# Two-block transformer kernel: split order of summed weight blocks on ScalarE, squares summed on VectorE, low parts ahead of adding DMAs

## Chip, cores and metric

One core of one Trainium2 chip runs the whole program in one launch. The metric is the device time of the program in microseconds (us), the median of several runs. TensorE (PE) does the matmuls, VectorE (DVE), ScalarE (ACT) and GpSimd (POOL) the elementwise work; SyncE (SP) and GpSimd issue DMAs. Each engine works through one queue of its own, in an order fixed when the program is built.

## What is computed

The reference runs two blocks of two layers each over x of 1 x 512 x 1024 in float32. For this change the feed-forward parts and the norms around them matter:

```python
# first block, each layer (sandwich norms)
h = h + rmsnorm(mixed, norm_gains[layer, 1])
hn = rmsnorm(h, norm_gains[layer, 2])
h = h + rmsnorm(swiglu_ffn(hn, ffn_w_in[layer], ffn_w_out[layer]), norm_gains[layer, 3])
# second block, each layer (norm ahead of each part)
x = x + mixer(rms_norm(x, mix_norm))
x = x + conv_ffn(rms_norm(x, ffn_norm[layer]), ffn_w_up[layer], ...)
```

The up-projection of each feed-forward part is 1024 x 5632, the down-projection 2816 x 1024. rmsnorm divides by the root of the mean square over the 1024 channels.

## The kernel before

**Layout.** Activations stand with channels on the 128 partitions: h is 128 x 8 x 512, eight chunks of channels by 512 tokens. Many steps work on half of the tokens (256) at a time; "half 0" and "half 1" below.

**Three matmuls for one.** Each fp32 operand is held as a high part (rounded to fp32r) and a low part (what the rounding left); a product is high x high + high x low + low x high. A weight block of 128 x 1024 is loaded into a buffer `raw0`, `raw1`, ... and split in `pump`: ACT casts it to the high part in a slot `W0` to `W3` (or `R0`, `X0`, ...), line 237, and DVE subtracts to get the low part, line 238.

**Seven products for eight.** The up-projection (`plan_up`, `product`, `up_first`, `up`) is done for each column pair j = 0 to 10 as seven products p = 1 to 7 over sums of quarter blocks, Strassen's way. Products 1 and 2 and product 3 of the early pairs take a quarter of the weights as loaded; 5, 6, 7 and 4 take sums. The sums are made in the raw buffer itself by adding DMAs: once the low part of a block is made, a GpSimd DMA with `accum_op=add` (line 240) adds the next quarter onto the same buffer, and the next block is split from it. So one buffer goes load, split, add, split, add, split. A block (j, p) is a `Spec`; `add` is the quarter that is to be added after its split. For pairs 0 to 3 the first sum, that of product 5, is not made behind a split but right after the load, by DMAs that `flush` issues (line 201).

**The order of the blocks.** `up_order` gives products 1 and 2 of pairs 0 to 3 first (eight products, run in `up_first`), then (0,5) (1,5) (0,3) (1,3) (0,6) (1,6) (0,7) (1,7) (0,4) (1,4), then the same for pairs 2 and 3, then the steady part. Slot W3 takes block 0 of the buffer that held `ya`, half of the norm's y, and so is free when `combine` (below) has read ya for the last time.

**Norms.** `norm_chain` is a generator whose steps are set between the matmuls of other work: each `yield t` puts the next step t us of matmul columns later on a planned PE clock (`tick`, 2.4 columns per ns). In the two sandwich layers a chain has two norms in a row: `rstd` of the mixer's (or feed-forward's) output y, `spread` of the result over all partitions, then y is scaled and added to h (lines 433 and 434), ACT squares h (line 435), DVE adds some of the squares (line 437), and `rstd` runs again on h:

```python
parts = [a[:, i] for a in (sums, tmp) for i in range(2)]
...
for j in range(2):
    for i, a in enumerate(parts):
        nc.tensor.matmul(st[:, j : j + 1], a[:, j * P : (j + 1) * P], self.invn, ...)
```

Squares of chunks 0, 2, 4 are added pairwise on DVE, those of chunks 6 and 7 are left in `tmp`; the four 128 x 256 parts are summed over partitions by PE (line 399). `rstd` ends with a DVE add of epsilon (line 403) and a GpSimd power (line 405); `spread` (line 412) puts the result on PE again. Then `combine` forms the left operands of the seven products (s1 to s4 and others) on DVE and ACT, lines 467 to 509, in an order written out by hand.

Each of the two layers has such chains twice, for two halves each: in `sandwich_out` (before the up-projection, while `up_first` runs in half 1) and in `sandwich_ffn` (after the down-projection). That makes eight chains with two norms. The second block's stages (`pre_out`) have one norm per chain and no line 435.

**What orders the queues.** PE's order is that of the program text (`in_order`). On the other engines a list scheduler orders instructions at build time: of those that are ready by its own estimate it issues the one with the smallest priority number, which is its place in the text; `high_priority(n)` moves it n places ahead. `FIRST` is 200; the norms use 400. `issue_after(ins)` puts what it wraps behind `ins` in the queue of `ins`'s engine, with no wait for it to finish.

Of the kernel before, what the change touches and what calls it, by code (L numbers as in the profile page):

```python
# [17 lines left out]
P = 128  # L18
# [20 lines left out]
class Rows:  # L39


    def __init__(self, *parts):
        self.parts = parts
# [15 lines left out]
class Spec:  # L59
# [1 line left out]

    def __init__(self, tag, nk, nc, slots, early, raw, loads=(), prep=None, add=None, ends=()):
        self.tag, self.nk, self.nc, self.slots, self.early = tag, nk, nc, slots, early
        self.raw, self.loads, self.prep, self.add, self.ends = raw, loads, prep, add, ends


class Net:
# [147 lines left out]
    def pump(self, most=99):  # L217
        nc = self.nc
        for _ in range(most):
            if self.n_split == len(self.specs):  # L220
                break
            self.load_more()
            s = self.specs[self.n_split]
            slot = next((x for x in s.slots if x in self.free), None)
            if slot is None or any(k not in self.raws for k in s.loads):
                return
            if any(key in s.loads for key, *_ in self.adds):
                self.flush(self.last_pow)
            self.free.discard(slot)
            if s.prep:  # L230
                out, x, y, eng = s.prep
                getattr(nc, eng).tensor_add(self.raws[out][1], self.raws[x][1], self.raws[y][1])
            n = s.nk * s.nc
            reg = self.slot_at[slot]
            hi, lo = reg[:, :n], reg[:, 1024 : 1024 + n]
            raw = self.raws[s.raw][1][:, :n]
            nc.scalar.copy(hi, raw)  # L237
            (nc.gpsimd if s.early else nc.vector).tensor_sub(lo, raw, hi.bitcast(F32))  # L238
            if s.add is not None:
                nc.gpsimd.dma_start(raw.rearrange("p (k c) -> p k c", k=s.nk), s.add, accum_op=ALU.add)  # L240
            for k in s.ends:
                self.raw_free.append(self.raws.pop(k)[0])
            r = dict(k=s.nk)
            self.loaded[self.n_split] = Chunk(
                slot, hi.rearrange("p (k c) -> p k c", **r), lo.rearrange("p (k c) -> p k c", **r), s.nk)
            self.n_split += 1
        self.load_more()
# [142 lines left out]
            nc.scalar.activation(sq[:, :n], src, AF.Square)  # L390
            eng.tensor_add(acc[:, cols], acc[:, cols], sq[:, :n])  # L391

    def rstd(self, parts):

        nc = self.nc
        st = self.mbank()
        for j in range(2):
            for i, a in enumerate(parts):
                nc.tensor.matmul(st[:, j : j + 1], a[:, j * P : (j + 1) * P], self.invn, start=i == 0,
                                 stop=i == len(parts) - 1)  # L400
        with self.tc.high_priority(400):
            v = self.sm.tile([P, 2], F32, tag="v", name="v")
            nc.vector.tensor_scalar_add(v, st[:, 0:2], EPS)
            r = self.sm.tile([P, 2], F32, tag="r", name="r")
            self.last_pow = nc.gpsimd.tensor_tensor(r, v, self.mhalf[:, 0:2], ALU.pow)
        return r
# [9 lines left out]
    def norm_chain(self, acc, half, gain, pool=None, y=None, acc_y=None, work=None):  # L416


        nc = self.nc
        cols = slice(half * HS, (half + 1) * HS)  # L420
        if y is not None:
            yield 2.6
            r = self.rstd([acc_y[:, cols]])
            if half and work is not None:
                self.flush(self.last_pow)
            yield 2.0
            R = self.spread(r)[:, :HS].unsqueeze(1).to_broadcast([P, 2, HS])
            with self.tc.high_priority(400):
                sums = pool.tile([P, 2, HS], F32, tag="sums", name="sums", bufs=2)
                for c in range(0, NC, 2):  # L430
                    tmp = y[:, c : c + 2, cols]
                    hv = self.h[:, c : c + 2, cols]
                    nc.vector.tensor_mul(tmp, tmp, R)
                    (nc.vector.tensor_sub if work is None else nc.vector.tensor_add)(hv, hv, tmp)
                    nc.scalar.activation(tmp if c else sums, hv, AF.Square)
                    if c in (2, 4):
                        nc.vector.tensor_add(sums, sums, tmp)
            parts = [a[:, i] for a in (sums, tmp) for i in range(2)]
            yield 7.0
        else:  # L440
            yield 5.4 if half and work is not None else 2.6
            parts = [acc[:, cols]]
        r = self.rstd(parts)
        if half and work is not None:
            self.flush(self.last_pow)
        yield 1.4 if y is not None else 2.8 if half and work is not None else 2.0
        R = self.spread(r)
        with self.tc.high_priority(400):
            if work is not None:
                with self.tc.manual_schedule(engines={mybir.EngineType.DVE}):  # L450
                    self.combine(pool, work, half, gain, R)
                return
            for c in range(NC):
                tmp = self.nrm.tile([P, HS], F32, tag="tmp", name="tmp", bufs=3)
                nc.vector.scalar_tensor_tensor(tmp, self.h[:, c, cols], gain[:, c : c + 1], R[:, :HS], ALU.mult,
                                               ALU.mult)
                self.split(tmp, self.res(c, 0, half), self.res(c, 1, half))
# [293 lines left out]
    def plan_up(self, tag, w, engines=None):  # L751


        wv = w.rearrange("(k p) c -> p k c", p=P)
        W = ["W0", "W1", "W2", "W3"]
        early = [W[:3] + RS, RS + W[:3]]
        src = lambda j, r, c: wv[:, 4 * r : 4 * r + 4, c * FF + j * 256 : c * FF + (j + 1) * 256]
        a, b, c = {}, {}, {}
        first, rest = self.up_order()

        def load(j, r, c, add=None):
            return self.raw(src(j, r, c), 4, 256, True, add)

        def spec(j, p, raw, **kw):
            slots = early[j > 0] if (j, p) in first else W[:3] if (j, p) in rest[-3:] else W
            self.specs.append(Spec(tag, 4, 256, slots, False, raw, **kw))

        for j, p in first + rest:
            e = j < self.EARLY
            if p == 1:  # L770
                k = load(j, 0, 0)
                if e:
                    spec(j, p, k, loads=[k], ends=[k])
                else:
                    a[j] = k
                    spec(j, p, k, loads=[k], add=None if engines else src(j, 0, 1))
            elif p == 2:
                k = load(j, 1, 0)
                spec(j, p, k, loads=[k], ends=[k])
            elif engines:  # L780
                if p == 5:
                    if e:
                        a[j] = load(j, 0, 0)
                    b[j] = load(j, 0, 1)
                    spec(j, p, a[j], loads=[a[j], b[j]], prep=(a[j], a[j], b[j], engines[0]))
                elif p == 3:
                    c[j] = load(j, 1, 1)
                    spec(j, p, c[j], loads=[c[j]])
                elif p == 6:
                    spec(j, p, a[j], prep=(a[j], a[j], c[j], engines[1]))  # L790
                elif p == 7:
                    spec(j, p, b[j], prep=(b[j], b[j], c[j], engines[2]), ends=[b[j], c[j]])
                else:
                    k = load(j, 1, 0)
                    spec(j, p, a[j], loads=[k], prep=(a[j], a[j], k, engines[3]), ends=[a[j], k])
            elif p == 5:
                if e:
                    a[j] = load(j, 0, 0, src(j, 0, 1))
                spec(j, p, a[j], loads=[a[j]], add=src(j, 1, 1))
            elif p == 3:  # L800
                c[j] = load(j, 1, 1)
                last = j == NF // 2 - 1
                spec(j, p, c[j], loads=[c[j]], add=None if last else src(j, 0, 1), ends=[c[j]] if last else [])
                if last:
                    c[j] = load(j, 1, 1, src(j, 0, 1))
            elif p == 6:
                spec(j, p, a[j], add=src(j, 1, 0))
            elif p == 7:
                spec(j, p, c[j], loads=[c[j]], ends=[c[j]])
            else:  # L810
                spec(j, p, a[j], ends=[a[j]])
# [1333 lines left out]
```

## Time and profile before

| what | value |
|---|---|
| median of 3 runs | 2576.38 us (2574.99 to 2578.72) |
| the profiled execution's own time | 2584.16 us |
| its span, first to last instruction | 2582.3 us |
| PE busy | 2467.4 us (96% of the span) |
| DVE / ACT / POOL busy | 1527.4 / 1168.2 / 550.1 us |
| mean granted TensorE clock | 0.98 of full speed |

Times in the trace are counted from the first instruction of the profiled execution. "Idle before" is time in which an engine stood still ahead of an instruction, with what ended it. The granted clock is a share of 2.4 GHz: 0.50 is 1.2 GHz, 1.00 is 2.4 GHz, and a value between them a stretch that had both.

### The profile page before, as it was taken

To read this page: it belongs to the slowest core of one execution; us is meant where nothing else is said; L and a number is where in the kernel's file an instruction comes from. 1 tells how busy PE (TensorE), PEld (TensorE's weight loads), DVE (VectorE), ACT (ScalarE), POOL (GpSimd) and SP (SyncE) were. 2 spreads that over 40 slices of the span, in tenths; PEclk is the share of its full clock that TensorE was granted. 3 is DMA by queue.
4 is the path that set the end of the run, shared out by engine and by line. 5 is a ranking of instruction groups with operands and counts; after the bars stand their busy time and mean duration, and the time that the engine had idled before them with its cause. 6 is when DMAs were issued, how large, how long until landed. Compare 5 with 4: busy or idle time off the path is not lost.

```text
span 2582.3 us, 40752 instructions
## 1 busy us (share of the span) xinstructions
PE 2467.4 (96%) x16477; PEld 2205.8 (85%) x16477; DVE 1527.4 (59%) x2400; ACT 1168.2 (45%) x1920; POOL 550.1 (21%) x500
## 2 busy tenths in 40 slices
PE   8999889999999998799999989899999999999999
PEld 6778889998898988799988759899888768989978
DVE  5766565563555555655625675787834445697841
ACT  4545445553232324455533553566622433466731
POOL 0000133310011111233101221455300000264400
PEclk9999989999999999899999999999999999999999
DMA  4223379944112123799531213989541223889741
GB/s 136 83 74 99 105 136 191 184 108 127 50 58 74 58 90 94 142 191 186 111 127 62 65 58 106 160 172 175 119 129 57 65 58 106 181 167 177 146 142 29
DMA packets 304886, 297.00 MB, mean 115 GB/s; under 512 B 11645, under 2 KB 294875, under 8 KB 304699
## 3 DMA queue, kind: packets, MB, share of 16 engines
q1 hardware_dynamic: 210235, 197.57, 25.0%
q0 software_dynamic: 94384, 96.81, 24.1%
q8 instruction: 129, 2.11, 0.3%
q14 instruction: 58, 0.48, 0.1%
q10 hardware_dynamic: 80, 0.03, 0.0%
HBM read 292.24 MB, written 2.13 MB: 114 GB/s over the span
## 4 chain that ended last, share of the span: by engine, by line
PE 43%; DVE 6%; DMA 3%; issue 3%; ACT 2%; POOL 1%; ACTq 0%; DVEq 0%; POOLq 0%
PE g L334 34%; PE a L334 4%; DMA raw<-in_ffn_w_up_dram 3%; DVE W L238 2%; ACT W L237 1%; PE m L334 1%; PE m L1900 1%; DVE u L932 1%; DVE s L932 1%; DVE s L933 0%; ACT s L931 0%; PE a L1883 0%; PE a L1209 0%; DVE R L173 0%; DVE u L933 0%
## 5 line engine op out<-in xcount | busy, mean ns | idle before, releaser
L238 DVE TENSOR_TENSOR W<-raw,W 128x1024 fp32r<-128x1024 f32 x455 | 573.2, 1263 | 458.9 <-ACT W L237 456.1
L237 ACT CAST W<-raw 128x1024 fp32r<-128x1024 f32 x455 | 472.4, 1040 | 603.6 <-PE g L334 272.7
L334 PE MATMUL g<-R,W 128*128 128x512 f32 (+2 forms) x3048 | 685.0, 375 | 7.8 <-DVE W L238 4.8
L334 PEld LDWEIGHTS g<-R,W 128*128 128x128 f32 (+1 forms) x3048 | 511.4, 190 | 105.1 <-issue 6.1
L334 PE MATMUL g<-s,W 128*128 128x256 f32 x3840 | 479.2, 284 | 27.6 <-ACT hid L947 13.6
L334 PEld LDWEIGHTS g<-s,W 128*128 128x128 f32 x3840 | 467.9, 191 | 32.5 <-ACT hid L947 16.5
L334 PE MATMUL g<-W,R 128*128 128x256 f32 (+1 forms) x1224 | 233.9, 337 | 0.0
L334 PEld LDWEIGHTS g<-W,R 128*128 128x128 f32 x1224 | 181.8, 191 | 25.3 <-issue 6.7
L334 PE MATMUL a<-a,W 128*128 128x256 f32 x1536 | 196.1, 283 | 3.5 <-DVE c L841 2.2
L334 PEld LDWEIGHTS a<-a,W 128*128 128x128 f32 x1536 | 188.8, 190 | 4.3 <-DVE c L841 2.4
L240 POOL DMA_DIRECT2D raw<-in_ffn_w_in_dram x78 | 100.4, 1289 | 228.5 <-DVE W L238 212.4
L240 POOL DMA_DIRECT2D raw<-in_ffn_w_up_dram x78 | 103.5, 1368 | 121.5 <-DVE W L238 114.5
L334 PE MATMUL g<-a,W 128*128 128x256 f32 x864 | 109.6, 282 | 0.3
L965 POOL TENSOR_TENSOR hid<-u,s 128x512 f32<-128x512 f32 x44 | 82.6, 1887 | 118.4 <-ACT s L962 111.8
L334 PE MATMUL g<-R,R 128*128 128x256 f32 (+1 forms) x792 | 107.0, 291 | 0.7 <-ACT ya L657 0.7
L334 PEld LDWEIGHTS g<-a,W 128*128 128x128 f32 x864 | 105.6, 189 | 1.1 <-DVE a L475 0.9
L238 DVE TENSOR_TENSOR X<-raw,X 128x1024 fp32r<-128x1024 f32 (+1 forms) x46 | 49.6, 1085 | 95.6 <-ACT X L237 95.6
L391 POOL TENSOR_TENSOR acc<-acc,sq 128x512 f32<-128x512 f32 x19 | 30.0, 1581 | 355.1 <-ACT sq L390 355.0
L334 PEld LDWEIGHTS g<-R,R 128*128 128x128 f32 x792 | 101.2, 195 | 2.7 <-ACT ya L657 1.1
L334 PE MATMUL g<-R,X 128*128 128x256 f32 (+1 forms) x576 | 94.0, 320 | 0.0
L334 PEld LDWEIGHTS g<-R,X 128*128 128x128 f32 x576 | 83.1, 190 | 7.8
L237 ACT CAST X<-raw 128x1024 fp32r<-128x1024 f32 (+1 forms) x46 | 42.9, 937 | 98.6 <-PE g L334 72.3
(413 smaller groups left out, 3451.2 us busy)
## 6 DMA issues: line engine op xcount, KB each, us to landing
raw<-in_ffn_w_in_dram POOLq DMA_DIRECT2D x88, 512.0 KB, 6.3
raw<-in_ffn_w_up_dram POOLq DMA_DIRECT2D x88, 512.0 KB, 6.3
raw<-in_ffn_w_in_dram SPq DMA_DIRECT2D x76, 512.0 KB, 4.9
raw<-in_ffn_w_up_dram SPq DMA_DIRECT2D x76, 512.0 KB, 4.8
raw<-in_ffn_w_out_dram SPq DMA_DIRECT2D x40, 512.0 KB, 3.5
raw<-in_ffn_w_down_dram SPq DMA_DIRECT2D x40, 512.0 KB, 4.0
raw<-in_hgrn_w_in_dram SPq DMA_DIRECT2D x32, 512.0 KB, 4.1
raw<-in_fox_w_in_dram SPq DMA_DIRECT2D x24, 512.0 KB, 3.8
```

The source lines that it names most:

```text
L237: nc.scalar.copy(hi, raw)
L238: (nc.gpsimd if s.early else nc.vector).tensor_sub(lo, raw, hi.bitcast(F32))
L240: nc.gpsimd.dma_start(raw.rearrange("p (k c) -> p k c", k=s.nk), s.add, accum_op=ALU.add)
L334: self.nc.tensor.matmul(*args, **kw, **(dict(skip_group_check=True) if skip else {}))
L391: eng.tensor_add(acc[:, cols], acc[:, cols], sq[:, :n])
L932: nc.vector.scalar_tensor_tensor(u[:, 1:], src[:, : S - 1], w(1), u[:, 1:], ALU.mult, ALU.add)
L965: nc.gpsimd.tensor_mul(hid[:, t], u, s)
L1900: mm(po[i * 64 : i * 64 + 64, h * HS : (h + 1) * HS], q[:, 2 * b + h, ck * 64 : (ck + 1) * 64], state[h], start=True, stop=True)
```

## The change

Three edits. First, every block of an up-projection is marked `up`, and those of products 4 to 7 `summed`; the high part of a summed block is put on ACT behind the last `up` high part that was traced before it, or behind the last square of the norm's half 1 in `sandwich_out`, whichever was traced later. Second, the low part of a block that an adding DMA follows gets priority 200. Third, `norm_chain` adds all squares on DVE (chunk 6's too, then the two columns of `sums` into one 128 x 256 accumulator), and `rstd` takes that one operand.

```diff
@@ Spec
+        self.up, self.summed = up, summed
@@ pump
-            nc.scalar.copy(hi, raw)
-            (nc.gpsimd if s.early else nc.vector).tensor_sub(lo, raw, hi.bitcast(F32))
+            with self.tc.issue_after(self.last_hi.ins) if s.summed else ExitStack():
+                hi_made = nc.scalar.copy(hi, raw)
+            if s.up:
+                self.last_hi = hi_made
+            with self.tc.high_priority(self.FIRST) if s.add is not None else ExitStack():
+                (nc.gpsimd if s.early else nc.vector).tensor_sub(lo, raw, hi.bitcast(F32))
@@ rstd
-    def rstd(self, parts):
+    def rstd(self, acc):
...
-            for i, a in enumerate(parts):
-                nc.tensor.matmul(st[:, j : j + 1], a[:, j * P : (j + 1) * P], self.invn, start=i == 0,
-                                 stop=i == len(parts) - 1)
+            nc.tensor.matmul(st[:, j : j + 1], acc[:, j * P : (j + 1) * P], self.invn, start=True, stop=True)
@@ norm_chain
-                    nc.scalar.activation(tmp if c else sums, hv, AF.Square)
-                    if c in (2, 4):
+                    square = nc.scalar.activation(tmp if c else sums, hv, AF.Square)
+                    if c:
                         nc.vector.tensor_add(sums, sums, tmp)
-            parts = [a[:, i] for a in (sums, tmp) for i in range(2)]
+                nc.vector.tensor_add(acc[:, cols], sums[:, 0], sums[:, 1])
+            if half and work is not None:
+                self.last_hi = square
@@ plan_up
-            self.specs.append(Spec(tag, 4, 256, slots, False, raw, **kw))
+            self.specs.append(Spec(tag, 4, 256, slots, False, raw, up=True, summed=p > 3, **kw))
```

## Rows read from the trace of the kernel before

**Rows 1.** The page: busy time, share of the span, instructions.

```profile
PE 2467.4 (96%) x16477; PEld 2205.8 (85%) x16477; DVE 1527.4 (59%) x2400; ACT 1168.2 (45%) x1920; POOL 550.1 (21%) x500
```

**Rows 2.** Busy time by stretch: PE, PEld, DVE, ACT, POOL; clock, DMA share, GB/s.

```profile
283.00:345.00 62.00, 49.62 (x354) 48.90 (x353) 38.65 (x71) 26.49 (x48) 8.88 (x9) 0.83 0.62 145
...
1600.00:1900.00 300.00, 283.55 (x2079) 269.25 (x2078) 230.87 (x264) 173.07 (x235) 123.06 (x81) 0.98 0.78 162
```

**Rows 3.** PE in order of time, first layer: start, busy, line, tiles, [idle before].

```profile
318.57 1.84 PE L334 MATMUL g<-a,R 128*128 128x256 f32 x14
328.66 0.98 PE L399 MATMUL m<-invn,sums 128*128 128x1 f32 x4 [8.25 <-DVE sums L437]
...
332.07 2.48 PE L334 MATMUL g<-a,R 128*128 128x256 f32 x10
...
335.20 1.05 PE L412 MATMUL m<-ident,r 128*128 128x128 f32 x4
335.91 3.22 PE L334 MATMUL a<-a,R 128*128 128x256 f32 x20
...
344.65 0.52 PE L334 MATMUL m<-s,W 128*128 128x256 f32 x3
```

**Rows 4.** ACT in order of time, the same stretch.

```profile
322.08 1.04 ACT L237 CAST W<-raw 128x1024 fp32r<-128x1024 f32 x1 [12.84 <-DMA raw<-in_ffn_w_in_dram]
...
325.46 0.61 ACT L435 ACTIVATE sums<-h 128x512 f32<-128x512 f32 x1
...
326.50 1.13 ACT L435 ACTIVATE yb<-h 128x512 f32<-128x512 f32 x2
```

**Rows 5.** DVE in order of time, the same stretch.

```profile
316.74 1.29 DVE L434 TENSOR_TENSOR h<-h,yb 128x512 f32<-128x512 f32 x2
323.16 1.23 DVE L238 TENSOR_TENSOR W<-raw,W 128x1024 fp32r<-128x1024 f32 x1 [5.14 <-ACT W L237]
...
327.83 0.68 DVE L437 TENSOR_TENSOR sums<-sums,yb 128x512 f32<-128x512 f32 x1
332.24 0.16 DVE L403 TENSOR_SCALAR v<-m 128x2 f32<-128x2 f32 x1 [3.73 <-PE m L399]
336.29 0.87 DVE L467 SCALAR_TENSOR_TENSOR ya<-h,gcol,m 128x256 f32<-128x256 f32 x2 [3.89 <-PE m L412]
```

**Rows 6.** POOL, the same stretch, and its adding DMAs as a group.

```profile
311.05 2.69 POOL L201 DMA_DIRECT2D raw<-in_ffn_w_in_dram  x2
...
332.49 0.71 POOL L405 TENSOR_TENSOR r<-v,mhalf 128x2 f32<-128x2 f32 x1 [6.53 <-DVE v L403]
...
L240 POOL DMA_DIRECT2D raw<-in_ffn_w_in_dram x78 | 100.4, 1289 | 228.5 <-DVE W L238 212.4 <-DMA raw<-in_ffn_w_in_dram 12.2 <-DVE hid L920 1.9
```

**Rows 7.** The norm's matmuls elsewhere: two on the timeline, two stretches, total waits.

```profile
294.93 0.58 PE L399 MATMUL m<-invn,sums 128*128 128x1 f32 x4 [2.78 <-DVE sums L437]
...
1041.21 0.98 PE L399 MATMUL m<-invn,sums 128*128 128x1 f32 x4 [7.97 <-DVE sums L437]
...
328.66:332.07 3.41, 3.41 (x17) 0.50 0.48 79
698.38:700.09 1.71, 1.71 (x19) 1.00 0.00 0
...
  DVE sums L437: 26.4, 7
```

**Rows 8.** Start of the first up-projection: PE, then ACT, on the timeline.

```profile
354.64 0.51 PE L334 MATMUL m<-s,W 128*128 128x256 f32 x2 [1.28 <-ACT W L237]
...
370.02 7.50 PE L334 MATMUL g<-s,W 128*128 128x256 f32 x48 [2.90 <-ACT hid L906]
...
347.59 1.05 ACT L237 CAST W<-raw 128x1024 fp32r<-128x1024 f32 x1 [0.74 <-PE m L334]
...
353.55 1.99 ACT L237 CAST W<-raw 128x1024 fp32r<-128x1024 f32 x2 [0.84 <-DVE s L475]
...
367.49 1.99 ACT L237 CAST W<-raw 128x1024 fp32r<-128x1024 f32 x2 [7.50 <-DMA raw<-in_ffn_w_in_dram]
```

More of the change, by code (lines that the diff above doesn't have):

```diff
@@ L59, with __init__ @@
 class Spec:
-    def __init__(self, tag, nk, nc, slots, early, raw, loads=(), prep=None, add=None, ends=()):
+    def __init__(self, tag, nk, nc, slots, early, raw, loads=(), prep=None, add=None, ends=(), up=False,
+                 summed=False):
         self.tag, self.nk, self.nc, self.slots, self.early = tag, nk, nc, slots, early
         self.raw, self.loads, self.prep, self.add, self.ends = raw, loads, prep, add, ends
+        self.up, self.summed = up, summed
 class Net:
@@ L422, in norm_chain @@
             yield 2.6
-            r = self.rstd([acc_y[:, cols]])
+            r = self.rstd(acc_y[:, cols])
             if half and work is not None:
@@ L441, in norm_chain @@
             yield 5.4 if half and work is not None else 2.6
-            parts = [acc[:, cols]]
-        r = self.rstd(parts)
+        r = self.rstd(acc[:, cols])
         if half and work is not None:
```

## The prediction

> **What bounds the kernel now.** I read the page first: PE is busy 96% of the span, DVE 59%, ACT 45%, POOL 21% [rows 1]. So a change can only pay where PE stands still, where it runs at the lower clock, or where it has fewer matmuls to do. Next came the table by stage, to find such places. In the 62 us around the norm ahead of the first up-projection PE is busy 49.6 us, and the mean granted clock is 0.83 [rows 2]. Third, PE in order of time there: its products end at 318.57 + 1.84 = 320.41, then it waits 8.25 us for the sum of the squares, and the norm's sixteen small matmuls follow [rows 3]. The second layer has the same picture at 1041.21 with 7.97 us [rows 7]; these two are the longest waits of PE in the trace.
>
> Fourth, who is late. DVE has finished h at 316.74 + 1.29 = 318.03 [rows 5], so the squares could start as its pieces come. But ACT starts the first square at 325.46. Before that it stood 12.84 us, to 322.08, ahead of a weight cast that waited for a DMA [rows 4]. This is the cast of block (0,5), the first summed one: its adding DMA was issued by POOL at 311.05 [rows 6] and took 322.08 - 311.05 = 11.0 us to release the cast. The squares need nothing from this DMA; they only stand behind the cast in ACT's queue.
>
> **The change part by part.**
>
> *The squares go ahead of the cast.* By the text of the kernel, does the cast fall behind the square? On the planned clock a product is 24 x 256 / 2400 = 2.56 us. The squares are traced 2.6 + 2.0 = 4.6 us into the eight first products. The cast of (0,5) needs the W slot that the second product gives back, at 5.12 us, so it is traced after the squares and is queued behind them. I count on that; a rival below covers that it is not so.
>
> Then: h at 318.03, the last square 0.61 us later [rows 4], about 318.7 with the hand-over; a sum of 0.69 (0.68 in [rows 5]) ends at 319.4. The added 128 x 256 sum has no row of its own: at most that 0.69, at least half of it, taken as 0.5. That gives 319.9, before PE comes free at 320.41. The wait of 8.25 goes.
>
> *The norm's matmuls.* Four operands become one, so 16 records become 4. Sixteen take 3.41 us at clock 0.50 and 1.71 us at 1.00 [rows 7]. After a wait of 8 us they ran at 0.50; without it the four should take a quarter of 1.71, 0.43, and end at 320.85.
>
> *What is late next.* Between the norm's matmuls and `spread` PE has 14 matmuls, 332.07 to 335.20 at the lower clock [rows 3], so about half of that, 1.6 us, at full clock: PE reaches `spread` at 322.4. It needs the result of line 403 on DVE and line 405 on POOL, 332.24 to 332.49 + 0.71 = 333.20, so 0.96 us [rows 5, 6]. Here the moved cast counts. The DMA lands when it did, so cast and low part stay where they are: 322.08, then 323.16 to 324.39 on DVE [rows 4, 5]. In ACT's queue the cast now stands right behind the last square, since the scheduler thought its data ready before the squares even in the kernel before. Its low part then reaches the scheduler just after the last sum and before the norm's matmuls have come back from PE, so I expect it in DVE's queue ahead of line 403. In the real run line 403 then starts at 324.4, not 320.9. With 0.96 us behind it, `spread` can start at 325.4; with the block's adding DMA issued first on POOL (1.29 us [rows 6]), at 326.7. Middle: 326.0, a new wait of 3.6 us.
>
> From `spread` at 335.20 to the first product of the up-projection at 344.65 are 9.45 us [rows 3], part of it at the lower clock; after 3.6 us of standing still I keep this number. The product then starts at 335.45 in place of 344.65: 9.2 us gained. `combine` starts 336.29 - 335.20 = 1.09 us after `spread` as before [rows 3, 5], so nothing behind it moves against PE. The second layer: its wait is 0.28 shorter, so 8.9. Together 18.1 us.
>
> *The other six chains with two norms.* They lose 12 records each: 0.75 x 1.71 = 1.3 us at full clock or 0.75 x 3.41 = 2.6 us at half. They get 0.69 + 0.5 = 1.2 us more DVE work behind the last square, which is on the path where PE waits already (the waits on line 437 sum to 26.4 us in 7 places, 16.2 of it in the two above [rows 7]) and hidden where it doesn't. So each gains between 0.1 and 2.6 us. I take 1.0, between them because both clocks occur: 6 us, bounds 0.6 and 15.6.
>
> *The queue order in the rest of the up-projections.* The cast at 353.55 waits for `combine` to leave slot W3 (released by DVE line 475), so it is that of (1,3); the slots W0 to W2 went round without it, and the cast at 347.59 is (0,6), which follows (1,3) in the list [rows 8]. The change forbids this overtaking: (0,6) goes from 347.59 to about 354.5. For it: the low part of (1,3), on which PE waits at 354.64 and after, goes up one place, 1.2 us. Against it: the adding DMA behind (0,6) leaves some 6 to 7 us later, and its sum is the last block of the pair, (0,4). PE's cover for that is the products of (1,6), (0,7) and (1,7), about 9 us. I take the two as cancelling, with the loss bounded in a rival.
>
> *Low parts first.* 78 adding DMAs follow a split in the two stages of the first block [rows 6]; the second block's two are planned alike, so 156 in all. In most turns DVE waits for the cast, not the DMA for DVE, so priority finds nothing to overtake: zero, with a rival.
>
> **The DMA's time and the Trainium skill.** The row has 11.0 us from issue to the cast [rows 4, 6]. The Trainium skill, "DMA: Bandwidth & Descriptors", section "Anatomy of one DMA — SWDGE (gpsimd) path", fits a GpSimd DMA as 2.0 us plus bytes over 436 GB/s, which is an estimate of 3.2 us for these 512 KB. By it the cast would never have held up the squares, and the sum would be the 6 us of the other chains alone. The trace disagrees by a factor of three on this very DMA, so the rule gets no chance of its own here.
>
> **Sum.** 18.1 + 6 = 24.1 us off the profiled execution's 2584.16 gives 2560.1. That execution was 7.8 us above the median of the runs, so in their terms 2576.38 - 24.1 = 2552.3: I predict 2552.
>
> **The rivals.**
>
> *A, no new wait.* If line 403 gets ahead of the low part, or the sum lands 3 us sooner, `spread` starts at 322.4 and the 72 matmuls up to the first product run at full clock: 4 take 0.4, and 68 between half of 3.13 and 1.84 per 14 [rows 3], so 7.6 to 8.9, middle 8.2; the product starts at 331.0. That is 13.7 us a layer, 27.1 for both, and with the 6 it makes 2543. For it: line 403 has priority 400 and the low part 200. Against it: priority only counts among what is ready, and line 403 isn't yet. Chance 0.2.
>
> *B, given back in the up-projections.* (0,6)'s late sum holds the cast of (0,4) in ACT's queue, and behind it stand the copies of line 906 on which PE already waits 2.90 us behind such a cast at 367.49 [rows 8]. If some 3 us of the 6 to 7 come through in each of four stages: 12 us back, 2564. For it: ACT did queue those copies behind two casts. Against it: the cover of three products. Chance 0.2.
>
> *C, slower.* The low parts with priority take 1.23 us each [rows 5] and go ahead of the convolution's and gate's DVE work, whose results ACT and then PE need; DVE is busy 231 of 300 us in the third up-projection [rows 2]. Each low part that comes through costs PE 1.2 us; twenty eat the gain of 24, and from twenty-four of the 156 the kernel is slower by more than 0.2%. At thirty: 2552 + 37 = 2589. Against it: PE is busy 283.6 of 300 us there, so most of such shifts are covered now. Chance 0.05.
>
> *D, the cast is not moved behind the squares.* Then only the 6 us are left: 2570, a little more than 0.2% faster, or no change if the added sums cost what they save. Chance 0.05.
>
> **How the numbers follow.** The forecast has 0.5, at 2552; the rivals 0.2, 0.2, 0.05, 0.05. Two in ten left out: from 2540 (A with 3 us more from the other chains) to 2566 (B and 2 us). About 0.2%, 5.2 us, is what a measurement of this kernel can tell from no change. Forecast, A and nearly all of B are faster by more, and part of D: 0.88. C gives 0.05 slower, and the rest, 0.07, is no change.
>
> **What would show it.** Line 399's records fall by 8 x 12 = 96, DVE's instructions rise from 2400 to 2416. At both places ahead of the up-projections the wait on the sum of squares is under 1 us and ACT's squares come before the cast that waits for the DMA. Right in detail: a wait of 3 to 4 us has come up at line 412, with line 238 ahead of line 403 on DVE. Wrong in the direction of A: none there. Wrong in the direction of B: waits on line 906 or 947 longer than 2.90 at the start of the up-projections. Wrong altogether: the cast still stands ahead of the squares, or PE waits in the third and fourth up-projections have grown by more than 20 us in all.

## The result and the profile after

| | before | after |
|---|---|---|
| median, same chip | 2578.06 us, 5 runs (2574.99 to 2586.27) | 2560.01 us, 5 runs (2556.42 to 2567.21) |
| profiled execution, its span | 2584.16, 2582.3 us | 2567.21, 2565.4 us |
| mean granted TensorE clock | 0.980 | 0.982 |

The ratio is 0.9927, 95% interval [0.9912, 0.9943]: 18.8 us faster (0.0073 x 2578), between 14.7 and 22.7. The prediction had 24.1 us off and 2552, with a range of 2540 to 2566. In the new kernel the lines have moved: 399 is 404, 403 is 407, 405 is 409, 412 is 416; the cast 237 is 240, the low part 238 is 244, its adding DMA 240 is 246, the flush 201 is 203; the squares 435 are 439, the sums 437 are 441, and the added sum is 442; the copies 906 and 947 are 911 and 952.

The busy line of the page after, beside [rows 1]:

```profile
PE 2452.7 (96%) x16381; PEld 2192.2 (85%) x16381; DVE 1535.5 (60%) x2416; ACT 1167.5 (46%) x1920; POOL 547.1 (21%) x500
```

PE has 96 records fewer and DVE 16 instructions more, as forecast. PE in order of time at the norm ahead of the first up-projection, beside [rows 3]:

```profile
319.33 1.84 PE L340 MATMUL g<-a,R 128*128 128x256 f32 x14
324.72 0.99 PE L404 MATMUL m<-invn,acc 128*128 128x1 f32 x4 [3.55 <-DVE acc L442]
...
328.70 1.05 PE L416 MATMUL m<-ident,r 128*128 128x128 f32 x4
...
338.30 8.71 PE L340 MATMUL m<-s,W 128*128 128x256 f32 x72
...
348.59 2.90 PE L340 MATMUL m<-s,W 128*128 128x256 f32 x22 [0.76 <-DVE W L244]
...
359.47 2.75 PE L340 MATMUL g<-s,W 128*128 128x256 f32 x21 [2.29 <-ACT hid L911]
```

From the last product before the norm to the first product of the up-projection were 344.65 - 318.57 = 26.08 us [rows 3]; now they are 338.30 - 319.33 = 18.97, so 7.1 us are gained where 9.2 were forecast. The wait on the sum has shrunk from 8.25 to 3.55 us, but it is not gone, and `spread` waits for nothing. ACT and then DVE show why; first ACT, beside [rows 4]:

```profile
316.70 0.59 ACT L845 COPY c<-g 128x512 f32<-128x512 f32 x1 [6.73 <-PE g L340]
317.31 1.28 ACT L904 ACT_TABLE_LOAD   x1
318.60 0.64 ACT L904 ACTIVATE c<-c 128x512 f32<-128x512 f32 x1
319.14 0.62 ACT L439 ACTIVATE sums<-h 128x512 f32<-128x512 f32 x1
...
320.18 1.14 ACT L439 ACTIVATE yb<-h 128x512 f32<-128x512 f32 x2
321.23 1.03 ACT L240 CAST W<-raw 128x1024 fp32r<-128x1024 f32 x1
```

The squares do come before the cast of (0,5). They end at 321.32 all the same, 2.6 us after the 318.7 of the forecast. Of this, 0.75 is a shift that PE's products share: h was complete at 318.78, 0.75 later than before. The other 1.9 come from ACT's queue, where a copy, a table load and a silu of the first pairs stand ahead of the squares. They stood there before the change as well, between the cast and the first square of [rows 4]:

```profile
323.63 1.28 ACT L899 ACT_TABLE_LOAD   x1
324.93 0.63 ACT L899 ACTIVATE c<-c 128x512 f32<-128x512 f32 x1
```

DVE, beside [rows 5]:

```profile
321.52 0.68 DVE L441 TENSOR_TENSOR sums<-sums,yb 128x512 f32<-128x512 f32 x1
322.29 1.23 DVE L244 TENSOR_TENSOR W<-raw,W 128x1024 fp32r<-128x1024 f32 x1
323.43 0.68 DVE L441 TENSOR_TENSOR sums<-sums,yb 128x512 f32<-128x512 f32 x1
324.15 0.42 DVE L442 TENSOR_TENSOR acc<-sums 128x256 f32<-128x256 f32 x1
325.74 0.16 DVE L407 TENSOR_SCALAR v<-m 128x2 f32<-128x2 f32 x1 [1.17 <-PE m L404]
```

The low part of (0,5) at 322.29 stands ahead of the *third* sum of squares, 323.43. Before the change there was no third sum. In this layer the adding DMA itself is no longer in the way: the cast at 321.23 follows the squares with no wait ahead of it, and what the low part takes from the norm is its own 1.23 us on DVE. Line 407, where the prediction had the low part in the way, comes later still and is free.

In the second layer the DMA is in the way again, now by way of DVE's queue. The cast waits 1.10 us for it, DVE stands 1.29 us ahead of the low part, and the third sum comes after both (ACT, then DVE):

```profile
1022.01 1.04 ACT L240 CAST W<-raw 128x1024 fp32r<-128x1024 f32 x1 [1.10 <-DMA raw<-in_ffn_w_in_dram]
```

```profile
1023.09 1.23 DVE L244 TENSOR_TENSOR W<-raw,W 128x1024 fp32r<-128x1024 f32 x1 [1.29 <-ACT W L240]
```

The wait on the sum there is 4.76 us, against 7.97 [rows 7]. One of the six other chains has a longer wait than before, and so has a copy at the start of the second up-projection (PE in order of time):

```profile
297.03 0.98 PE L404 MATMUL m<-invn,acc 128*128 128x1 f32 x4 [4.17 <-DVE acc L442]
...
1025.52 0.98 PE L404 MATMUL m<-invn,acc 128*128 128x1 f32 x4 [4.76 <-DVE acc L442]
...
1062.46 6.80 PE L340 MATMUL g<-s,W 128*128 128x256 f32 x33 [4.95 <-ACT hid L911]
```

At 297.03 PE waits 4.17 us where it waited 2.78 [rows 7], 1.39 more: the added sums are on the path there. Finally, over the whole span after, the total of the waits on the sum (beside the last line of [rows 7]), and PE's waits on the copies of the first block's and the second block's up-projections (line and releaser, us in total, times, longest):

```profile
  DVE acc L442: 26.4, 9
```

```profile
PE g L340 <- ACT hid L952: 15.4, 14, 3.6
PE g L340 <- ACT hid L911: 8.5, 3, 4.9
```

The total of the waits on the sum is the same 26.4 us as before, though the two long ones fell from 16.2 to 8.3: the others grew from 10.2 to 18.1.

### The profile page after: what moved, and what is told of

Its sections match the earlier page's. It is cut to its first block, busy times and chain, and to the rows that moved or that the text cites. A ratio compares the mean times of both kernels' runs of the same rounds, so it can differ in the third digit from the quotient of the medians.

```text
span 2565.4 us, 40579 instructions
## 1 busy us (share of the span) xinstructions
PE 2452.7 (96%) x16381; PEld 2192.2 (85%) x16381; DVE 1535.5 (60%) x2416; ACT 1167.5 (46%) x1920; POOL 547.1 (21%) x500
## 4 chain that ended last, share of the span: by engine, by line
PE 78%; DVE 6%; issue 5%; DMA 4%; ACT 4%; POOL 2%; ACTq 0%; SPq 0%; POOLq 0%; DVEq 0%
PE g L340 62%; PE a L340 7%; DMA raw<-in_ffn_w_up_dram 2%; DVE W L244 2%; PE m L340 1%; ACT W L240 1%; DMA raw<-in_ffn_w_in_dram 1%; PE a L1214 1%; POOL raw L246 1%; PE a L1459 1%; PE m L1459 1%; PE a L1501 1%; PE m L1905 1%; ACT s L936 0%; PE g L1254 0%
```

## The experiments

Each kernel was timed against the kernel before on the same chip. The table has the ratio of the times, and from the profiled executions how much later (-: sooner) PE comes through four stretches than before: the two norms (from the product at 318.57 to 344.65, and from 1031.40 to 1057.57, the same places of the second layer, times of before), and the starts of the two up-projections behind them (344.65 to 377.36, 1057.57 to 1088.60). Where nothing was changed that bears on a stretch, two executions still differ by up to 1.4 us, as e2_prio shows, and more where a DMA lands sooner: at norm 2 of e3_sums the cast came 8.6 us after its adding DMA was issued, and 10.7 us in the kernel before.

| kernel | ratio, 95% interval | norm 1 | norm 2 | up 1 | up 2 |
|---|---|---|---|---|---|
| the change | 0.9927 [0.9912, 0.9943] | -7.1 | -6.4 | -4.2 | +1.2 |
| e1_order: edit 1 alone | 0.9901 [0.9888, 0.9914] | -7.8 | -9.2 | -2.5 | -1.0 |
| e2_prio: edit 2 alone | 1.0005 [0.9989, 1.0022] | -0.4 | -1.4 | -0.4 | +0.2 |
| e3_sums: edit 3 alone | 1.0012 [1.0000, 1.0024] | -0.9 | -4.4 | -1.5 | +1.7 |
| e4_no_prio: without edit 2 | 0.9925 [0.9912, 0.9938] | -5.2 | -6.4 | -4.4 | -1.3 |
| e5_p5: edit 1 for product 5 only | 0.9961 [0.9945, 0.9976] | -7.3 | -6.4 | -2.0 | +0.8 |
| e6_low_behind_sum | 0.9906 [0.9893, 0.9919] | -5.9 | -9.6 | -1.7 | +0.4 |
| e7_low_behind_norm | 0.9897 [0.9878, 0.9916] | -9.6 | -9.7 | -3.1 | -0.6 |
| e8_silu_behind | 0.9892 [0.9871, 0.9913] | -12.5 | -12.6 | -2.2 | -1.2 |
| e9_no_sums | 0.9883 [0.9865, 0.9901] | -12.4 | -12.5 | -2.4 | -1.2 |
| e10_copies_ahead | 0.9997 [0.9984, 1.001] | -12.5 | -12.1 | -0.3 | +0.6 |
| e11_copies_no_sums | 0.9975 [0.9964, 0.9985] | -12.4 | -12.5 | -1.1 | -0.5 |

**One edit at a time.** The theory after the result: edit 3 makes the sum into which the low part pushes itself, so edit 1 alone does better than all three. The rival: the wait is the late squares' doing, and edit 1 alone has it too.

e1_order, the kernel before with the first edit:

```diff
-            nc.scalar.copy(hi, raw)
+            with self.tc.issue_after(self.last_hi.ins) if s.summed else ExitStack():
+                hi_made = nc.scalar.copy(hi, raw)
+            if s.up:
+                self.last_hi = hi_made
...
+            if half and work is not None:
+                self.last_hi = square
...
```

> Only the first edit: summed blocks queued on ScalarE behind the squares and behind the up blocks before them; squares summed and low parts prioritised as before. Theory 1 (in the changed kernel the low part of block (0,5) stands on DVE ahead of the third sum of squares, and that sum exists only since the third edit, so the norm waits for the DMA through it): here the norm's matmuls need only the second sum, PE waits 1 to 2 us there in both sandwich layers instead of 3.55 and 4.76, and each of these two places gains 8 to 10 us against the kernel before; ratio 0.991 to 0.993, as good as the whole change. Rival (the remaining wait comes from the squares and sums themselves, not from the low part): waits of 3 to 5 us as in the changed kernel and no saving of matmuls, ratio 0.994 to 0.996.

e2_prio, with the second:

```diff
-            (nc.gpsimd if s.early else nc.vector).tensor_sub(lo, raw, hi.bitcast(F32))
+            with self.tc.high_priority(self.FIRST) if s.add is not None else ExitStack():
+                (nc.gpsimd if s.early else nc.vector).tensor_sub(lo, raw, hi.bitcast(F32))
```

> Only the second edit: the low parts that an adding DMA follows get priority 200. The prediction put this at nothing. The changed kernel without it differs from the changed kernel by less than the intervals, so: ratio 0.998 to 1.002, the waits of about 8 us ahead of the up-projections unchanged. Rival C of the prediction (low parts ahead of the convolution's work cost PE time) would show as 1.003 or more, with longer waits on ScalarE's copies in the third and fourth up-projections.

e3_sums, with the third:

```diff
-                    if c in (2, 4):
+                    if c:
                         nc.vector.tensor_add(sums, sums, tmp)
+                nc.vector.tensor_add(acc[:, cols], sums[:, 0], sums[:, 1])
...
+            nc.tensor.matmul(st[:, j : j + 1], acc[:, j * P : (j + 1) * P], self.invn, start=True, stop=True)
```

> Only the third edit: all squares summed on VectorE, one operand for the norm's matmuls. The prediction's step had 1 us for each of six chains, and the two at the long waits would gain about 2 more each because 12 matmuls at the lower clock go and 1.2 us of sums come: 8 us, ratio 0.997. From the changed kernel's trace, where the six other chains together gave about 2 us, I expect 3 to 5 us, ratio 0.998 to 0.999. In both the waits of about 8 us stay and grow to about 9.

e4_no_prio, the changed kernel without the second:

```diff
-            with self.tc.high_priority(self.FIRST) if s.add is not None else ExitStack():
-                (nc.gpsimd if s.early else nc.vector).tensor_sub(lo, raw, hi.bitcast(F32))
+            (nc.gpsimd if s.early else nc.vector).tensor_sub(lo, raw, hi.bitcast(F32))
```

> The changed kernel without the second edit (low parts keep their own priority). If the priority put the low part of (0,5) ahead of the third sum of squares, the waits of 3.55 and 4.76 us at the norm go and the kernel is 6 to 10 us faster than with it. If that place comes from the cast's place behind the squares, the waits stay, and only the up-projections can change: within 5 us of the changed kernel, ratio to the kernel before 0.991 to 0.995.

Edit 1 alone has 0.9901, better than the whole; the two intervals only touch. Edit 2 is nothing that these runs can tell from zero, in either direction, and without it the waits at the norm stay (5.46 and 4.85 us; at the first the cast waited 1.79 us for its DMA). Edit 3 alone is no gain and perhaps 3 us of loss, where 3 to 5 us of gain were expected. PE and DVE of e1_order at the first norm:

```profile
321.16 0.58 PE L404 MATMUL m<-invn,sums 128*128 128x1 f32 x4 [1.13 <-DVE sums L442]
321.60 0.60 PE L404 MATMUL m<-invn,yb 128*128 128x1 f32 x4
322.06 0.99 PE L404 MATMUL m<-invn,sums 128*128 128x1 f32 x4
...
```

```profile
320.33 0.68 DVE L442 TENSOR_TENSOR sums<-sums,yb 128x512 f32<-128x512 f32 x1
323.39 1.22 DVE L243 TENSOR_TENSOR W<-raw,W 128x1024 fp32r<-128x1024 f32 x1 [2.37 <-ACT W L240]
324.53 0.15 DVE L408 TENSOR_SCALAR v<-m 128x2 f32<-128x2 f32 x1
```

Here is the very order that the prediction described, the low part behind the last sum and ahead of epsilon. It makes no wait at `spread` here, for the 3.6 us of the forecast, because PE is busy meanwhile: with sixteen matmuls, the second eight of them at half clock, until 323.77, and with the fourteen products behind them, also at half clock, until 327.0.

**The low part out of the way.** Theory: each place that the low part leaves gives back what it held up. e6_low_behind_sum sets it behind line 442, e7_low_behind_norm behind line 407; e8_silu_behind also sets the silu of the early pairs behind the squares on ACT.

```diff
 e6, pump (low_after is the norm's last sum)
-            with self.tc.high_priority(self.FIRST) if s.add is not None else ExitStack():
+            first = self.tc.high_priority(self.FIRST) if s.add is not None else ExitStack()
+            behind = self.tc.issue_after(self.low_after.ins) if s.summed and self.low_after else ExitStack()
+            with first, behind:
                 (nc.gpsimd if s.early else nc.vector).tensor_sub(lo, raw, hi.bitcast(F32))
 ...
 e7: the same with low_after the add of epsilon, and (0,5) traced behind it
+        if self.held:
+            self.held, self.low_after = False, self.last_v
+            self.pump()
 ...
 e8: as e7, and in swiglu_evac
-                nc.scalar.activation(c, c, AF.Silu)
+                with self.tc.issue_after(self.last_square.ins):
+                    nc.scalar.activation(c, c, AF.Silu)
```

> The changed kernel with one order more: on DVE the low part of a summed block is put behind the last sum of squares. Theory 1: the norm's matmuls then wait under 2 us in both places (the squares end at about 321.3 and two sums follow), the rest of the norm runs at the higher clock, 4 to 6 us a layer more than the changed kernel: ratio 0.988 to 0.991. If line 407 behind the low part then waits for the DMA, as the prediction said, a wait of 1 to 3 us appears at spread and half of that is lost again. Rival (sums themselves are the wait): waits and time as in the changed kernel, ratio 0.9927.

> The changed kernel, with block (0,5) traced after the norm's second set of matmuls and its low part put on DVE behind line 407 (the epsilon). In the first sandwich layer the kernel with the low part behind the last sum waits 2.4 us at the norm and 0.65 at spread, where the epsilon stands behind the low part and the power behind the adding DMA on POOL. Theory 1: the 2.4 us stay (they come from squares that start late, behind the table load and the silu on ScalarE), the wait at spread goes; 0.5 to 2 us a layer more than that kernel, ratio 0.989 to 0.991. Rival (the norm's wait is still the cast's DMA): no wait at all at the norm.

> The kernel before this one in the list, and the silu of the first pairs (with its table load of 1.28 us) put behind the squares on ScalarE as well. If the squares are late because of the table load and the silu, 1.9 us, the wait at the norm falls from 2.4 to under 1 us in both layers, the clock holds, and 2 to 4 us a layer come on top: ratio 0.986 to 0.989. If not, the same as that kernel.

PE at the first norm, first e6_low_behind_sum, then e8_silu_behind:

```profile
322.59 0.91 PE L407 MATMUL m<-invn,acc 128*128 128x1 f32 x4 [2.44 <-DVE acc L445]
...
327.34 1.22 PE L419 MATMUL m<-ident,r 128*128 128x128 f32 x4 [0.65 <-POOL r L412]
```

```profile
317.51 1.84 PE L343 MATMUL g<-a,R 128*128 128x256 f32 x14
320.40 0.58 PE L407 MATMUL m<-invn,acc 128*128 128x1 f32 x4 [1.06 <-DVE acc L445]
...
331.12 5.15 PE L343 MATMUL m<-s,W 128*128 128x256 f32 x42
```

With the low part behind the sum the wait falls from 3.55 to 2.44, and a wait at `spread` comes up, as the prediction had it, of 0.65 us. The first norm as a whole takes 1.2 us longer than in the change all the same (-5.9 for -7.1): the twenty matmuls behind `spread` took 4.61 us there, 3.37 in the change. In the second layer no such wait came up, and e6 has -9.6. In e7 the wait at `spread` is gone, and 2.44 stays: the late squares and the added sums. In e8, with the table load and the silu out of the way, it is 1.06. There the squares end at 317.69, and DVE's sums behind them at 320.25. The norm takes 331.12 - 317.51 = 13.6 us of 26.1, all of it at full clock:

```profile
317.50:331.12 13.62, 12.56 (x106) 12.39 (x105) 11.25 (x21) 7.62 (x11) 3.49 (x4) 1.00 1.17 246
```

In the times of the whole kernel the 2.9 us in each of the two norms that e8 has over e7 don't show: 0.9892 and 0.9897 can't be told apart, and e8 just misses the 0.986 to 0.989 that was expected.

**Is the third edit worth anything, once the sums are free?** e9_no_sums is e8 without edits 2 and 3:

```diff
-            nc.tensor.matmul(st[:, j : j + 1], acc[:, j * P : (j + 1) * P], self.invn, start=True, stop=True)
+            for i, a in enumerate(parts):
+                nc.tensor.matmul(st[:, j : j + 1], a[:, j * P : (j + 1) * P], self.invn, start=i == 0,
+                                 stop=i == len(parts) - 1)
```

> First edit, with the low part of block (0,5) behind the epsilon of the norm on DVE and the silu of the first pairs behind the squares on ACT, but without the second and the third edit: four operands and sixteen matmuls in the norm again. Theory (the third edit costs as much as it saves once nothing stands in front of the sums): the ratio to the kernel before is that of the same version with the third edit, 0.989, within 0.002; the wait ahead of the norm's matmuls is near 0 in place of 1.06 and the norm's matmuls take 1.3 us longer. Rival (the twelve records saved are worth 1 us and more in each of eight chains once DVE is free): 0.992 to 0.994.

PE in e9_no_sums, the first and last of the four groups of the norm:

```profile
319.56 1.84 PE L341 MATMUL g<-a,R 128*128 128x256 f32 x14
321.24 0.53 PE L406 MATMUL m<-invn,sums 128*128 128x1 f32 x4
...
322.53 0.58 PE L406 MATMUL m<-invn,yb 128*128 128x1 f32 x4
...
333.26 6.93 PE L341 MATMUL m<-s,W 128*128 128x256 f32 x57
```

No wait at all, sixteen matmuls at full clock in 322.98 - 321.24 = 1.7 us, and the norm in 333.26 - 319.56 = 13.7 us, as long as in e8. The theory holds as far as these runs can tell: the difference between 0.9883 and 0.9892 is well inside the two intervals, which leave room for some 7 us either way. e9 has the lowest ratio of the study, with a median of 2550.38 us.

**What the 3.55 us were made of.** The waits ahead of the first norm's matmuls, taken together, divide them. Without the low part in the way 2.44 are left (e7), so it cost 1.1. With neither the low part nor the added sums in the way 1.13 are left (e1_order), so the added sums cost 1.3. With the table load and the silu out of the way too, nothing is left (e9), so the late squares cost 1.1. In the second layer the same three are 2.3, 1.3 and 1.2 of 4.76 us.

**The queue order in the rest of the up-projections.** The prediction had this at nothing. e5_p5 keeps the new order for product 5 alone, in the changed kernel:

```diff
-            self.specs.append(Spec(tag, 4, 256, slots, False, raw, up=True, summed=p > 3, **kw))
+            self.specs.append(Spec(tag, 4, 256, slots, False, raw, up=True, summed=p == 5, **kw))
```

> The changed kernel with only the blocks of product 5 queued (behind the squares, and behind the up block before them); products 6, 7 and 4 keep the scheduler's order. The norm is as in the changed kernel. If the fixed order behind (1,3) is what moved the start of the up-projections (4.2 us gained in the first, 1.2 us lost in the second), the waits there come back as before the change: 1.3, 1.9 and 2.9 us in each of the first two. Then this kernel is 3 us slower than the changed one in the first up-projection and about equal in the second: ratio 0.993 to 0.995. If the start moved because PE and the DMAs arrive there earlier, no difference from 0.9927 and no such waits.

It has 0.9961, outside the range that was expected, so the order of the other summed blocks is worth 0.0034, 8.8 us (with the two intervals, between 3 and 14). PE in e5_p5 at the first up-projection:

```profile
347.06 0.50 PE L340 MATMUL m<-s,W 128*128 128x256 f32 x2 [1.33 <-ACT W L240]
349.46 4.39 PE L340 MATMUL m<-s,W 128*128 128x256 f32 x22 [1.90 <-DVE W L244]
```

The cast and the low part of (1,3) hold PE 1.33 and 1.90 us, as before the change [rows 8]; with the whole edit they hold it 0.32 and 0.76. That is only a part of the 8.8: by the table the two starts differ by 2.2 and -0.4 us between e5_p5 and the change. The two profiled executions lie 5.8 us apart; 2.0 of this have come up by the `spread` at 1609 us in the kernel before, ahead of the third up-projection, and 5.4 by the one at 1960, behind it, so 3.4 lie there. What makes them there was not taken apart.

**The copies behind a late cast.** Rival B's place is the wait on a copy at 359.47 and 1062.46 in the profile after. e10_copies_ahead is e8 with the copies of products 5, 6 and 7 ahead of the next summed cast on ACT; to get this order a weight slot is also given back only when its product's copy has been traced, so casts are traced later, for every product and in both blocks. e11_copies_no_sums does the same to e9:

```diff
 up
-                self.product(tag, p, z[j])
+                ch = self.product(tag, p, z[j], keep=True)
...
+            self.release(ch)
             done.add((j, p))
 swiglu_evac, and so in conv_evac
-                nc.scalar.copy(out[1], two(ps))
+                self.last_hi = nc.scalar.copy(out[1], two(ps))
```

> The whole change with the low part of (0,5) behind the norm's epsilon and the silu behind the squares, and in the up-projections the copies out of PSUM of products 5, 6 and 7 go ahead of the next cast on ACT: a slot is given back behind its product's copy, and a summed cast stands behind the last copy. Theory (the waits of 2.93 and 3.50 us at the start of the first two up-projections are copies that stand behind a cast whose adding DMA is late, rival B of the prediction): both go, ratio 0.9892 - 0.0025 = 0.987, or 0.985 if the second block's two gain as much. Rival (the cast waited for is itself needed by PE next): the two waits come back one or two products later at a cast or a low part, and the ratio stays at 0.989.

> The same copies ahead of casts on the version without the second and third edits. Theory (the third edit pays nothing, the copies pay 2.5 us and more a stage): the ratio of the version with the third edit and the copies ahead, within 0.002: 0.985 to 0.988. Rival: the third edit pays by itself, and this is 0.002 or more above it.

Both lose: 0.9997 where e8 has 0.9892, 0.9975 where e9 has 0.9883. So the theory falls. At the first up-projection the copy no longer holds PE, but PE waits for a cast instead: the second of two in a row, of which the first waited 4.45 us for a DMA (e10_copies_ahead, PE and ACT):

```profile
346.61 0.79 PE L343 MATMUL m<-s,W 128*128 128x256 f32 x2 [5.67 <-ACT W L241]
```

```profile
344.56 1.99 ACT L241 CAST W<-raw 128x1024 fp32r<-128x1024 f32 x2 [4.45 <-DMA raw<-in_ffn_w_in_dram]
```

In the second block the copies themselves became the wait; line 962 there is line 959 of e8. The groups of waits, first of e8_silu_behind, then of e10_copies_ahead:

```profile
PE g L343 <- ACT hid L959: 17.2, 14, 3.7
...
PE g L343 <- ACT hid L961: 2.0, 3, 0.8
```

```profile
PE g L343 <- ACT hid L962: 21.1, 12, 5.4
...
PE g L343 <- ACT hid L964: 12.8, 4, 3.8
```

The rival was right that PE needs a cast next; the 0.989 that it gave was missed as well, since the second block loses too. By the two profiled executions, 35.5 us apart where the ratios give 27, the first block costs e10 12 us against e8 up to the third up-projection, and the second 23 more. Why the second loses more was not taken apart, and no run parts the new order of the copies from the later return of the slots.

## Why the prediction was right, point by point

Sign, size and range were right: 18.8 us of 24.1, 2560 in 2540 to 2566. That the sum of the terms came out so near is in part luck: the two norms and the six other chains gave 4.6 and some 9 us less than forecast, and a term that was put at nothing gave 8.8.

- **The squares ahead of the cast**: right. In every kernel with edit 1 the cast stands behind the last square, and with edit 1 alone the 8.25 us are 1.13. Rival D fell.
- **"The wait of 8.25 goes"**: the step that failed; 3.55 and 4.76 us are left. The prediction had the squares end 0.61 us after h, and they ended 2.5 us after it (0.7 in e8, where load and silu are behind them): the copy, the table load and the silu that stand between cast and squares in ACT's queue were in the trace before the change, in the 2.3 us between the cast's end at 323.12 and the first square at 325.46 [rows 4], and it did not ask what they were. With squares so late the added sums of edit 3, which it priced by their own durations and hid behind PE's products, are on the path. And it asked only whether the low part would stand ahead of line 403, not whether it would stand ahead of the sums that the edit itself adds. In the first layer the three cost 1.1 (squares), 1.3 (sums) and 1.1 us (low part), in the second 1.2, 1.3 and 2.3. In the time of the whole norm, the lower clock included, e7 and e8 put the low part at 2.5 and 3.3 us in the two layers and the table load with the silu at 2.9 in each (differences of the table's rows).
- **The new wait of 3.6 us at `spread`**: wrong as a place in the change, where `spread` waits for nothing. It exists in e6, at 0.65 us. In the change PE still waited for the sum when the low part was done. The two norms gave 7.1 + 6.4 = 13.5 us for the forecast's 18.1.
- **Rival A**, no wait and full clock, 13.7 us a layer: its premise did not come, but e8 and e9, which make it true, gain 12.4 to 12.6 us in each layer, at a granted clock of 1.00.
- **The six other chains at 1 us each**: mis-sized. Edit 3 in all eight chains measures 1.0012, a cost of 3 us, with 0 to 6 in its interval. Where PE waits already, the added DVE steps make the wait longer (1.39 us at 297.03, and 18.1 for 10.2 in all the places but the two long ones); the times show no gain from the twelve records beyond that.
- **The queue order in the rest of the up-projections at nothing**: mis-sized too, on the other side, 8.8 us by e5. The half "for it" came through (the low part of (1,3) goes up a place). Of the half against it, rival B, something came as well: PE's waits on line 911 sum to 8.5 us for 5.6 before, one of them is 4.95 where 2.90 was the longest [rows 8], and line 952 has one of 3.6. That is the sign that the prediction gave for B. It is the smaller half.
- **Low parts first at nothing**: right, by e2 and e4. Rival C fell with it.

The terms as measured, 13.5 - 3 + 8.8 = 19.3 us, stand beside the 18.8; the 3 us count again some of what the two norms already hold, and the 8.8 have an interval of 3 to 14, so the agreement is closer than the terms are known. By the same terms edit 1 alone has 7.8 + 9.2 + 8.8 = 25.8, and 25.5 was measured (0.0099 x 2578).

On the adding DMA that started all this, the trace after agrees with [rows 4, 6]: the two that POOL issued in the 13 us ahead of the norm took a median of 10.9 us to land, in the view of DMAs there.

```profile
raw<-in_ffn_w_in_dram POOLq DMA_DIRECT2D x2, 512.0 KB, 10.9
```

The fit of the Trainium skill, "DMA: Bandwidth & Descriptors", section "Anatomy of one DMA — SWDGE (gpsimd) path", gives an estimate of 3.2 us for this size; the measurement decides here again.

## What to carry to other kernels

A late transfer holds up whatever stands behind it in any queue it passes: the cast on ACT before the change, the low part on DVE in the second layer after it, the DMA issue on POOL in e6. When one of these is cleared, look at the next queue for the same late data, and at the instructions that the change itself adds, since those are the ones that the old trace does not show in the way. And read every instruction between the late one and the one that it holds up: here 2.3 us of other ACT work stood between them, and the cast's move left that work where it was. Work taken off PE and put on the engine that PE is waiting for pays nothing; here sixteen small matmuls with no wait and four behind a wait of 1.06 us took the same time.

## What the runs showed of the hardware that was not expected

The granted clock at the norm fell in one kernel and not in two others that differ little. In e8 PE waited 1.06 us and then ran four small matmuls, in e9 it ran sixteen without a wait, and in both the clock stayed at 1.00, 2.4 GHz. In e1_order, with a wait of 1.13 us and then sixteen, the first eight took 0.58 and 0.60 us, and from 322.06 on a group took 0.99: 1.2 GHz, and it stayed there through the next fourteen products (e1_order):

```profile
323.77 2.48 PE L339 MATMUL g<-a,R 128*128 128x256 f32 x10
326.05 1.05 PE L339 MATMUL a<-a,R 128*128 128x256 f32 x4
```

In the second layer of e1_order PE waited 1.18 us, and there all four groups of the sixteen took 0.58; the clock fell only in the products behind them, of which ten took 1.93 us (1.44 in e8) and the next four 1.05:

```profile
1022.71 0.58 PE L404 MATMUL m<-invn,sums 128*128 128x1 f32 x4 [1.18 <-DVE sums L442]
...
1024.49 1.93 PE L339 MATMUL g<-a,R 128*128 128x256 f32 x10
```

In the first layer, from the product before the norm to the first product of the up-projection, e1_order takes 18.28 us, e9 13.70. PE stood still for 1.13 us of it and for no more (busy 17.34 of 18.47):

```profile
318.00:336.47 18.47, 17.34 (x119) 17.00 (x119) 10.68 (x19) 7.67 (x13) 3.45 (x4) 0.82 0.92 180
```

So of the 4.58 us between the two the wait is 1.13, and the lower clock behind it the other 3.45: three times the wait. In the second layer the two are 3.2 us apart (16.92 and 13.71), with 1.4 of waits (1.18, and 0.19 at `spread`) and 1.8 at the lower clock. Whether it takes the sixteen matmuls behind the wait, or only the 0.07 to 0.12 us more of it than in e8, these runs don't tell apart.
